# Evictions of the attention pass at a higher scheduler priority, with the copies of a key or query bank grouped ahead of its subtractions

## The chip, the cores and the metric

The kernel runs on one core of one Trainium2 chip. Its time is the device time in microseconds of one execution; 2264.72 us is the median of 3 runs (2261.97 to 2266.19). One execution was profiled by the hardware profiler; it took 2265.88 us, and its span, from the first recorded instruction to the last, is 2264.2 us.

## The reference

One layer of a hybrid encoder over 4096 tokens with 1024 channels. RMSNorm, one input projection, a group A of 4 heads (a matrix-memory recurrence in both directions), a group B of 8 query heads over 2 key/value heads (attention in a window of 128 tokens to either side), one output projection, a residual. Only group B is computed in the part of the kernel that the change touches:

```python
def windowed_gqa(q, k, v, sink, rel_bias):      # q [B,S,8,64], k, v [B,S,2,64]
    qb = q.reshape(bsz, nb, BLOCK, B_KV_HEADS, Q_PER_KV, B_HEAD_DIM)
    kw, vw = band(k), band(v)                   # the block before, this one, the next
    scores = jnp.einsum('bnqhgd,bnkhd->bnhgqk', qb, kw) * (B_HEAD_DIM ** -0.5)
...
    scores = jnp.where(mask[None, :, None, None], scores + bias, NEG_INF)
    m = jnp.maximum(jnp.max(scores, axis=-1), sink_l)
    p = jnp.exp(scores - m[..., None])
    denom = jnp.sum(p, axis=-1) + jnp.exp(sink_l - m)
    out = jnp.einsum('bnhgqk,bnkhd->bnqhgd', p, vw) / denom.transpose(0, 1, 4, 2, 3)[..., None]
```

## The kernel before

The kernel works in passes. Pass 1 (the first 700 us or so) normalizes and transposes x, projects queries, keys and values, and does the whole of the window attention; the passes behind it (the recurrence of group A, the output projection) are not touched by the change. At the end of pass 1 the weights of the next pass are loaded and split as well (`w2_load`), and the gates of group A are prepared (`gate1` to `gate3`).

Numbers are kept as a pair: a rounded high part and the rest as a low part, and products are three matmuls. So a TensorE result in a PSUM bank leaves it in two steps: ScalarE copies it (which rounds it, the high part), and VectorE subtracts that copy from the bank (the low part). This pair of steps is called an eviction here. Evictions of five kinds matter:

- xT (L358 copy, L359 subtraction): the transposed x, from the banks xtp.
- kk (L392, L393 copies, L394, L395 subtractions, each pair once for either key head): the keys, from kp. The program before writes copy, copy, subtraction, subtraction for head 0, then the same for head 1.
- vg (L415 copy, L416 addition): the values, from vp. From vg the value tile v is made (L419 on ScalarE, L420 on VectorE) and GpSimd adds the gate biases (L426).
- q (L449 copy, L450 subtraction, once for either half): the queries, from qp. Before: copy, subtraction, copy, subtraction.
- ab (L330 copy, L331 addition): the attention output, from op. After every second one a DMA stores ab to at_d, and there is one ab buffer.

The banks of xtp, kp, vp, qp and v2p come from one pool named pj of three PSUM banks, handed on from one tile to the next in the order in which they come free. A matmul that opens a new tile in a bank waits until the tile before in that bank has been evicted.

Attention itself, for each of 64 slots (a block of 128 queries by a key/value head): four pairs of score matmuls (sp, L276), VectorE adds the bias and takes the row maximum (L279, and L285 for the negated maximum), ScalarE takes four exponentials (L287) and one of the sink (L290), VectorE adds and inverts the row sums (L291, L292), GpSimd multiplies (L294), TensorE transposes the result (tp, L306), ScalarE and VectorE split it (pt, L308 and L309), and TensorE multiplies it with the values (op, L320).

What sets the order: the order of TensorE's instructions is that of the written program, in which `interleave` weaves the projections into the slots. The main loop runs 13 times (b = 0 to 12), each time four slots: first qproj of one block woven into two slots (the query half), then kproj and vproj of the next block and the transposes of a third woven into two slots (the key half). ScalarE, VectorE, GpSimd and the queue of SyncE, which issues most DMAs, get their order from the Tile scheduler: it takes, among the instructions that its own model says are ready, the one of highest priority, by default the earliest written. Each engine then works strictly through its list, and waits where an operand isn't there yet. If two engines touch one PSUM bank, the program lets one wait for the other.

`w2_load(j, c0)`, called three times near the end of pass 1, loads 8 tiles of weights through two staging buffers (tag xf) and splits each: most on ScalarE and VectorE (L470, L471), every fourth with GpSimd's help (L466 to L468). A staging buffer's next DMA goes out once its split has been done.

Of the kernel before, what the change touches and what calls it, by code (L numbers as in the profile page):

```python
# [12 lines left out]
AF = mybir.ActivationFunctionType  # L13
ALU = mybir.AluOpType
# [9 lines left out]
BIG = 1e30  # L24
BUCKET_STARTS = [0, 1, 2, 3, 4, 5, 6, 7, 8, 12, 16, 23, 32, 46, 64, 91]


def f32(ap):
    return ap.bitcast(F32)
# [133 lines left out]
def pass1(c):  # L163
    nc, tc, A = c.nc, c.tc, c.A
    NB = 16
    with ExitStack() as es:
# [144 lines left out]
        def att_o(sl, i):  # L311
            n, kv = sl // 2, sl % 2
# [5 lines left out]
            op, pt, vt = OP[sl], PT.pop((sl, i)), V[n - 1 + js[i]][:, kv, :]  # L318
# [7 lines left out]
            ab = AB[n]  # L326
            a = slice(0, 64) if kv == 0 else slice(64, 128)
            o = slice(64, 128) if kv == 0 else slice(0, 64)
            ov = op.rearrange("p (g q) -> p g q", g=4)
            nc.scalar.copy(ab[a], ov[o])  # L330
            nc.vector.tensor_add(ab[a], ov[a], ab[a])  # L331
# [14 lines left out]
        def transposes(b):  # L346
# [4 lines left out]
            def unit(kk):  # L351
# [6 lines left out]
                nc.scalar.copy(xt[:, :, 0, 2:], tp)  # L358
                nc.vector.tensor_tensor(out=xt[:, :, 1, 2:], in0=tp, in1=f32(xt[:, :, 0, 2:]), op=ALU.subtract)  # L359
# [13 lines left out]
        def kproj(b):  # L373
            R = {}

            def unit(k, j):
# [12 lines left out]
                for kv in range(2):  # L389
                    a = slice(kv * 64, kv * 64 + 64)  # L390
                    o = slice(64 - kv * 64, 128 - kv * 64)
                    nc.scalar.copy(kk[a, kv, 0, 256:512], kp[a, :])  # L392
                    nc.scalar.copy(kk[o, kv, 0, 256:512], kp[a, :])  # L393
                    nc.vector.tensor_sub(kk[a, kv, 1, 256:512], kp[a, :], f32(kk[a, kv, 0, 256:512]))  # L394
                    nc.vector.tensor_sub(kk[o, kv, 1, 256:512], kp[a, :], f32(kk[a, kv, 0, 256:512]))  # L395
# [3 lines left out]
        def vproj(b):  # L399
            R = {}  # L400

            def unit(i, k):
# [12 lines left out]
                nc.scalar.copy(vg, vp[:, 1, :])  # L415
                nc.vector.tensor_add(vg, vp[:, 0, :], vg)  # L416
# [14 lines left out]
        def qproj(b):  # L431
# [3 lines left out]
            def unit(m, k, j):  # L435
# [10 lines left out]
                for z in range(2):  # L446
                    a = slice(z * 64, z * 64 + 64)
                    o = slice(64 - z * 64, 128 - z * 64)
                    nc.scalar.activation(qt[a, z, :], qp[a, :], AF.Copy, scale=0.125)  # L449
                    nc.vector.scalar_tensor_tensor(qt[o, z, :], qp[a, :], 0.125, f32(qt[a, z, :]),  # L450
                                                   ALU.mult, ALU.subtract)
# [950 lines left out]
```

## Time and profile before

| | |
|---|---|
| median of 3 runs | 2264.72 us (2261.97 to 2266.19) |
| profiled execution, its own time | 2265.88 us |
| its span | 2264.2 us |
| TensorE (PE) busy in the span | 2210.4 us, 98% |
| VectorE (DVE) busy | 1492.3 us, 66% |
| ScalarE (ACT) busy | 1086.4 us, 48% |
| TensorE's share of the chain that ended last | 83% |
| granted TensorE clock, mean over the span | 0.995 |

The span is the time from the profiler's first event to its last; the execution's own time is 1.7 us more. Busy times are sums over all three passes, so the shares say little about one of them. In the rows below PE is TensorE's matmuls, PEld its weight loads, DVE VectorE, ACT ScalarE, POOL GpSimd, SP SyncE. A time in square brackets at the end of a row is how long the engine sat idle ahead of it, and what released it. "x4" at a row's end stands for four instructions of the same form that follow each other.

### The profile page before, as it was taken

To read this page: it belongs to the slowest core of one execution; us is meant where nothing else is said; L and a number is where in the kernel's file an instruction comes from. 1 tells how busy PE (TensorE), PEld (TensorE's weight loads), DVE (VectorE), ACT (ScalarE), POOL (GpSimd) and SP (SyncE) were. 2 spreads that over 40 slices of the span, in tenths; PEclk is the share of its full clock that TensorE was granted. 3 is DMA by queue.
4 is the path that set the end of the run, shared out by engine and by line. 5 is a ranking of instruction groups with operands and counts; after the bars stand their busy time and mean duration, and the time that the engine had idled before them with its cause. 6 is when DMAs were issued, how large, how long until landed. Compare 5 with 4: busy or idle time off the path is not lost.

```text
span 2264.2 us, 36115 instructions
## 1 busy us (share of the span) xinstructions
PE 2210.4 (98%) x12432; PEld 1914.0 (85%) x12432; DVE 1492.3 (66%) x3253; ACT 1086.4 (48%) x2710; POOL 617.2 (27%) x978
## 2 busy tenths in 40 slices
PE   7999999999989999999999999999999999999998
PEld 6999999999878888888887788888888888888887
DVE  5888888888877655655568554555554352766676
ACT  5777777777754333433345444434343331333332
POOL 2545454544532112211222111111111111122222
PEclk9999999999999999999999999999999999999999
DMA  8322222222225234432454986778676799466654
GB/s 235 122 98 99 99 99 99 98 99 80 74 86 159 88 109 152 157 109 88 155 191 132 311 244 226 212 232 254 222 223 200 268 365 311 148 168 167 167 169 129
DMA packets 257803, 376.08 MB, mean 166 GB/s; under 512 B 19507, under 2 KB 151219, under 8 KB 257620
## 3 DMA queue, kind: packets, MB, share of 16 engines
q1 hardware_dynamic: 238452, 307.90, 42.3%
q0 software_dynamic: 19024, 65.68, 9.5%
q8 instruction: 98, 1.61, 0.3%
q14 instruction: 85, 0.70, 0.1%
q10 hardware_dynamic: 144, 0.20, 0.0%
HBM read 253.18 MB, written 120.52 MB: 165 GB/s over the span
## 4 chain that ended last, share of the span: by engine, by line
PE 83%; DVE 7%; ACT 4%; DMA 3%; issue 2%; SPq 0%; POOL 0%; POOLq 0%; ACTq 0%; DVEq 0%
PE up L747 15%; PE o L1194 14%; PE op L1038 7%; PE zp L1038 7%; PE v2p L720 7%; PE qp L441 7%; PE zbp L153 3%; PE zbp L155 3%; PE zbp L154 3%; PE sp L276 3%; PE op L320 2%; PE tp L306 2%; PE num L991 2%; PE num L990 2%; ACT s L287 2%
## 5 line engine op out<-in xcount | busy, mean ns | idle before, releaser
L747 PE MATMUL up<-xb,w 128*128 128x512 f32 x1344 | 338.6, 396 | 0.0
L1194 PE MATMUL o<-wo,yo 128*128 128x512 f32 (+1 forms) x1356 | 312.1, 392 | 0.0
L1194 PEld LDWEIGHTS o<-wo,yo 128*128 128x128 f32 x1356 | 253.1, 188 | 59.1
L747 PEld LDWEIGHTS up<-xb,w 128*128 128x128 f32 x1344 | 243.9, 189 | 47.2
L294 POOL TENSOR_TENSOR s<-s,st 128x384 f32<-128x384 f32 (+1 forms) x256 | 203.9, 828 | 241.8 <-DVE st L292 191.1
L765 DVE SCALAR_TENSOR_TENSOR qk<-U,cw,qk 128x512 f32<-128x512 f32 x256 | 190.1, 755 | 93.0 <-ACT qk L763 89.2
L441 PE MATMUL qp<-xT,wqb 128*128 128x256 f32 x1536 | 248.3, 290 | 1.2 <-DVE xT L359 1.2
L441 PEld LDWEIGHTS qp<-xT,wqb 128*128 128x128 f32 x1536 | 221.8, 192 | 11.1 <-issue 1.7
L1038 PE MATMUL op<-w,xs 128*128 128x512 f32 x720 | 202.5, 408 | 1.1 <-DMA xs<-xT_d 1.1
L1038 PE MATMUL zp<-w,xs 128*128 128x512 f32 x720 | 187.9, 401 | 1.7 <-DVE z L1047 1.7
L287 ACT ACTIVATE s<-s,st 128x384 f32<-128x384 f32 (+1 forms) x256 | 152.9, 599 | 70.7 <-DVE st L285 70.7
L720 PE MATMUL v2p<-w,xb 128*128 128x512 f32 x672 | 157.2, 394 | 0.0
L1038 PEld LDWEIGHTS zp<-w,xs 128*128 128x128 f32 x720 | 130.7, 188 | 28.7 <-DVE z L1047 2.1
L720 PEld LDWEIGHTS v2p<-w,xb 128*128 128x128 f32 x672 | 126.1, 188 | 29.8 <-DMA xb<-xT_d 0.4
L1005 ACT ACTIVATE hs<-num,r 128x128 f32<-128x128 f32 x128 | 46.9, 367 | 209.6 <-DVE r L1002 171.5
L1038 PEld LDWEIGHTS op<-w,xs 128*128 128x128 f32 x720 | 126.5, 189 | 22.9 <-ACT hs L1005 1.6
L279 DVE CUSTOM_DVE_ANT_0 s<-sp,bias 128x384 f32<-128x384 f32 (+1 forms) x256 | 137.5, 541 | 12.5 <-PE sp L276 5.5
L276 PE MATMUL sp<-kk,q 128*128 128x384 f32 (+1 forms) x512 | 135.3, 345 | 2.1 <-DVE st L279 2.1
L309 DVE TENSOR_TENSOR pt<-tp,pt 128x512 fp32r<-128x512 f32 x188 | 128.2, 683 | 8.5 <-ACT pt L308 5.8
L320 PE MATMUL op<-pt,v 128*128 128x512 f32 x376 | 122.7, 408 | 6.2 <-DVE ab L331 5.8
L308 ACT CAST pt<-tp 128x512 fp32r<-128x512 f32 x188 | 109.1, 582 | 40.3 <-PE tp L306 37.3
L306 PE MATMUL tp<-ident,s 128*128 128x128 f32 x752 | 113.8, 273 | 2.5 <-DVE pt L309 2.0
(259 smaller groups left out, 4477.0 us busy)
## 6 DMA issues: line engine op xcount, KB each, us to landing
xT_d<-xT SPq DMA_DIRECT2D x128, 256.0 KB, 2.5
xc<-xT_d SPq DMA_DIRECT2D x64, 512.0 KB, 7.8
xs<-xT_d SPq DMA_DIRECT2D x120, 256.0 KB, 6.5
xb<-xT_d SPq DMA_DIRECT2D x48, 514.0 KB, 8.9
x<-x SPq DMA_DIRECT2D x32, 512.0 KB, 4.4
E<-m_d SPq DMA_DIRECT2D x64, 256.0 KB, 4.8
W<-w_d SPq DMA_DIRECT2D x64, 256.0 KB, 5.8
y<-y_d SPq DMA_DIRECT2D x32, 512.0 KB, 4.3
```

The source lines that it names most:

```text
L276: nc.tensor.matmul(sp[:, jl:jr], qt, kk[:, kv, z, col - 128 + jl:col - 128 + jr], start=(z == 0), stop=(z == 1))
L279: nc.vector.tensor_tensor_reduce(out=s[:, jl:jr], in0=sp[:, jl:jr], in1=bias[kv][:, g, jl:jr], op0=ALU.add, op1=ALU.max, scale=1.0, scalar ...
L287: nc.scalar.activation(ps[g][:, jl:jr], ps[g][:, jl:jr], AF.Exp, bias=ng[:, g:g + 1], accum_out=rs[:, g:g + 1])
L294: nc.gpsimd.tensor_tensor(out=ps[g][:, jl:jr], in0=ps[g][:, jl:jr], in1=rd[:, g:g + 1].broadcast_to([128, jr - jl]), op=ALU.mult)
L306: nc.tensor.transpose(tp[:, g * 128:(g + 1) * 128], ps[g][:, j * 128:(j + 1) * 128], c.ident)
L320: nc.tensor.matmul(op, vt, pt[:, z, :], start=(i == 0 and z == 0), stop=(i == len(js) - 1 and z == 1))
L441: nc.tensor.matmul(qp, wq[k // 2][:, k % 2, w, m * 128:m * 128 + 128], x[k], start=(k == 0 and j == 0), stop=(k == KT - 1 and j == 2))
L720: nc.tensor.matmul(vp, a, wv[k // 2][:, k % 2, m, :], start=(k == 0 and j == 0), stop=(k == KT - 1 and j == 2))
L747: nc.tensor.matmul(up[:, 0:hi - lo], w[k // 2][:, k % 2, a, cs], x, start=(k == 0 and j == 0), stop=(k == KT - 1 and j == 2))
L765: nc.vector.scalar_tensor_tensor(acc, U[:, t:t + 512], cw[:, cm, t:t + 1], acc, ALU.mult, ALU.add)
L1038: nc.tensor.matmul(P[nm], XS[n](a, k), w[:, m, :], start=(k == 0 and j == 0), stop=(k == KT - 1 and j == 2))
L1194: nc.tensor.matmul(p, a[:, z, k, :], w[k // 2][:, k % 2, m, lo:hi], start=k == 0 and z == 1, stop=k == 3 and z == 0 and m == 0)
```

## The change

The evictions ab, xT, kk, vg and q are written inside `tc.high_priority(offset=EV)` with EV = 400, which makes the scheduler rank them as if they had been written 400 places earlier. Further, the four ScalarE copies of a kk bank now come in front of its four VectorE subtractions, and the two copies of a q bank in front of its two subtractions. Instructions, shapes and the order on TensorE stay as they were.

```diff
+EV = 400
...
-            nc.scalar.copy(ab[a], ov[o])
-            nc.vector.tensor_add(ab[a], ov[a], ab[a])
+            with tc.high_priority(offset=EV):
+                nc.scalar.copy(ab[a], ov[o])
+                nc.vector.tensor_add(ab[a], ov[a], ab[a])
...
-                for kv in range(2):
-                    a = slice(kv * 64, kv * 64 + 64)
-                    o = slice(64 - kv * 64, 128 - kv * 64)
-                    nc.scalar.copy(kk[a, kv, 0, 256:512], kp[a, :])
-                    nc.scalar.copy(kk[o, kv, 0, 256:512], kp[a, :])
-                    nc.vector.tensor_sub(kk[a, kv, 1, 256:512], kp[a, :], f32(kk[a, kv, 0, 256:512]))
-                    nc.vector.tensor_sub(kk[o, kv, 1, 256:512], kp[a, :], f32(kk[a, kv, 0, 256:512]))
+                with tc.high_priority(offset=EV):
+                    for kv in range(2):
+                        a = slice(kv * 64, kv * 64 + 64)
+                        o = slice(64 - kv * 64, 128 - kv * 64)
+                        nc.scalar.copy(kk[a, kv, 0, 256:512], kp[a, :])
+                        nc.scalar.copy(kk[o, kv, 0, 256:512], kp[a, :])
+                    for kv in range(2):
+                        a = slice(kv * 64, kv * 64 + 64)
+                        o = slice(64 - kv * 64, 128 - kv * 64)
+                        nc.vector.tensor_sub(kk[a, kv, 1, 256:512], kp[a, :], f32(kk[a, kv, 0, 256:512]))
+                        nc.vector.tensor_sub(kk[o, kv, 1, 256:512], kp[a, :], f32(kk[a, kv, 0, 256:512]))
...
-                for z in range(2):
-                    a = slice(z * 64, z * 64 + 64)
-                    o = slice(64 - z * 64, 128 - z * 64)
-                    nc.scalar.activation(qt[a, z, :], qp[a, :], AF.Copy, scale=0.125)
-                    nc.vector.scalar_tensor_tensor(qt[o, z, :], qp[a, :], 0.125, f32(qt[a, z, :]),
-                                                   ALU.mult, ALU.subtract)
+                with tc.high_priority(offset=EV):
+                    for z in range(2):
+                        a = slice(z * 64, z * 64 + 64)
+                        o = slice(64 - z * 64, 128 - z * 64)
+                        nc.scalar.activation(qt[a, z, :], qp[a, :], AF.Copy, scale=0.125)
+                    for z in range(2):
+                        a = slice(z * 64, z * 64 + 64)
+                        o = slice(64 - z * 64, 128 - z * 64)
+                        nc.vector.scalar_tensor_tensor(qt[o, z, :], qp[a, :], 0.125, f32(qt[a, z, :]),
+                                                       ALU.mult, ALU.subtract)
```

The xT and vg evictions are only wrapped, as ab is. Lines of the changed kernel stand a little lower: L287 is L288, L290 is L291, L358 is L361, L392 and L393 are L396 and L397, L394 and L395 are L401 and L402, L449 is L458, L470 is L482.

The lists of the engines change with it. First ScalarE in the key half of one turn of the loop, before: kk_3734 is the key tile evicted here, kp_3627 its bank, s_0 to s_3 with st_3621 the four exponentials and the sums of one slot.

```order
L308 CAST pt_2_3729<-tp_2_3724 128x512
L392 CAST kk_3734<-kp_3627 64x256
L287 ACTIVATE s_0_3625,st_3621<-s_0_3625,st_3621 128x384
L287 ACTIVATE s_1_3640,st_3621<-s_1_3640,st_3621 128x384
L287 ACTIVATE s_2_3671,st_3621<-s_2_3671,st_3621 128x384
L287 ACTIVATE s_3_3697,st_3621<-s_3_3697,st_3621 128x384
L393 CAST kk_3734<-kp_3627 64x256
L290 ACTIVATE st_3621<-st_3621 128x4
L358 CAST xT_2_3772<-xtp_2_3767 128x2x256
L308 CAST pt_0_3782<-tp_0_3777 128x512
L415 COPY vg_3795<-vp_3750 128x144
L392 CAST kk_3734<-kp_3627 64x256
```

And the same place of ScalarE's list in the changed kernel:

```order
L309 CAST pt_2_3729<-tp_2_3724 128x512
L396 CAST kk_3734<-kp_3627 64x256
L397 CAST kk_3734<-kp_3627 64x256
L396 CAST kk_3734<-kp_3627 64x256
L397 CAST kk_3734<-kp_3627 64x256
L288 ACTIVATE s_0_3625,st_3621<-s_0_3625,st_3621 128x384
L288 ACTIVATE s_1_3640,st_3621<-s_1_3640,st_3621 128x384
L288 ACTIVATE s_2_3671,st_3621<-s_2_3671,st_3621 128x384
L288 ACTIVATE s_3_3697,st_3621<-s_3_3697,st_3621 128x384
L291 ACTIVATE st_3621<-st_3621 128x4
L361 CAST xT_2_3772<-xtp_2_3767 128x2x256
L309 CAST pt_0_3782<-tp_0_3777 128x512
```

The four copies of the key bank stood apart, one of them ahead of the slot's four exponentials and the others behind; now all four stand ahead of them.

VectorE at the same place, before:

```order
L309 TENSOR_TENSOR pt_2_3729<-tp_2_3724,pt_2_3729 128x512
L279 ISA s_5_3765,st_3744<-sp_5_3762,bias_326 128x384
L279 ISA st_3744 128x1
L394 TENSOR_TENSOR kk_3734<-kp_3627,kk_3734 64x256
L395 TENSOR_TENSOR kk_3734<-kp_3627,kk_3734 64x256
L291 TENSOR_TENSOR st_3621<-st_3621 128x4
L359 TENSOR_TENSOR xT_2_3772<-xtp_2_3767,xT_2_3772 128x2x256
L292 RECIPROCAL st_3621<-st_3621 128x4
L309 TENSOR_TENSOR pt_0_3782<-tp_0_3777,pt_0_3782 128x512
```

And in the changed kernel:

```order
L310 TENSOR_TENSOR pt_2_3729<-tp_2_3724,pt_2_3729 128x512
L401 TENSOR_TENSOR kk_3734<-kp_3627,kk_3734 64x256
L402 TENSOR_TENSOR kk_3734<-kp_3627,kk_3734 64x256
L401 TENSOR_TENSOR kk_3734<-kp_3627,kk_3734 64x256
L402 TENSOR_TENSOR kk_3734<-kp_3627,kk_3734 64x256
L280 ISA s_5_3765,st_3744<-sp_5_3762,bias_326 128x384
L280 ISA st_3744 128x1
L292 TENSOR_TENSOR st_3621<-st_3621 128x4
L293 RECIPROCAL st_3621<-st_3621 128x4
L362 TENSOR_TENSOR xT_2_3772<-xtp_2_3767,xT_2_3772 128x2x256
```

All four subtractions of the key bank now stand together, ahead of the score tile s_5 and of the transposed tile xT_2, which before came behind two of them. Which bank follows which changes too: the second value tile of a block (vp_3810 here) takes the bank of xtp_2 before, so that its first matmul waits for the xT_2 subtraction (L359); in the changed program it takes the bank of kp and waits for the last key subtraction (L402).

Last, ScalarE near the end of pass 1, where w_16 are weight tiles of `w2_load` whose data (w2s) come by DMA, and pt_2 belongs to the attention. Before:

```order
L470 ACTIVATE w_14_8845<-w2s_8851,nw 128x512
L330 COPY ab_8538<-op_8494 64x512
L308 CAST pt_2_8568<-tp_2_8563 128x512
L491 COPY v2t_8453<-v2p_8452 128x4x128
L470 ACTIVATE w_16_8855<-w2s_8856,nw 128x512
L555 ACTIVATE g_8581<-g_8581 128x256
```

And in the changed kernel:

```order
L309 CAST pt_1_8531<-tp_1_8526 128x512
L332 COPY ab_8538<-op_8494 64x512
L482 ACTIVATE w_16_8855<-w2s_8856,nw 128x512
L482 ACTIVATE w_16_8855<-w2s_8860,nw 128x512
L309 CAST pt_2_8568<-tp_2_8563 128x512
L503 COPY v2t_8453<-v2p_8452 128x4x128
```

Both splits of w_16 have moved ahead of the copy pt_2 (the second one stood behind four exponentials before). The same holds at two more places of this stretch: the second split of w_06 stands ahead of a pt_1 copy, and the first split of w_26 ahead of a v2t copy and the ab eviction that followed it.

## Rows read from the trace of the kernel before

**Rows 1.** The page: span, and busy time by engine.

```profile
span 2264.2 us, 36115 instructions
...
PE 2210.4 (98%) x12432; PEld 1914.0 (85%) x12432; DVE 1492.3 (66%) x3253; ACT 1086.4 (48%) x2710; POOL 617.2 (27%) x978
```

**Rows 2.** Busy time by stretch (stretch, length, engines, granted clock, DMA share, GB/s).

```profile
100.00:570.00 470.00, 461.55 (x3391) 439.00 (x3390) 413.24 (x1078) 352.05 (x946) 229.16 (x334) 1.00 0.28 94
570.00:700.00 130.00, 118.07 (x779) 105.67 (x778) 102.87 (x230) 79.63 (x187) 51.28 (x81) 0.97 0.25 78
```

**Rows 3.** Waits of all engines, 100 to 570 us (total us, times, longest).

```profile
DVE st L291 <- ACT st L290: 23.3, 25, 1.4
...
DVE kk L394 <- ACT kk L393: 8.1, 12, 0.7
PE vp L410 <- DVE xT L359: 7.5, 12, 0.6
...
PEld op L320 <- DVE ab L331: 3.1, 13, 0.7
```

**Rows 4.** TensorE in order of time, in one turn (start, us, what).

```profile
305.39 0.51 PE L276 MATMUL sp<-kk,q 128*128 128x384 f32 x2
305.74 0.52 PE L382 MATMUL kp<-xT,wkv 128*128 128x256 f32 x3
...
316.35 0.56 PE L276 MATMUL sp<-kk,q 128*128 128x384 f32 x2
317.55 0.40 PE L410 MATMUL vp<-wkv,xT 128*128 128x288 f32 x1 [0.64 <-DVE xT L359]
```

**Rows 5.** VectorE in order of time, same key half.

```profile
314.01 0.69 DVE L309 TENSOR_TENSOR pt<-tp,pt 128x512 fp32r<-128x512 f32 x1
...
315.85 0.42 DVE L394 TENSOR_TENSOR kk<-kp,kk 64x256 fp32r<-64x256 f32 x1 [0.68 <-ACT kk L393]
...
316.81 0.68 DVE L359 TENSOR_TENSOR xT<-xtp,xT 128x512 fp32r<-128x512 f32 x1
...
320.39 0.69 DVE L420 TENSOR_TENSOR v<-vg,v 128x128 fp32r<-128x128 f32 x1
...
322.68 0.67 DVE L359 TENSOR_TENSOR xT<-xtp,xT 128x512 fp32r<-128x512 f32 x1
```

**Rows 6.** ScalarE in order of time, same key half.

```profile
312.14 0.36 ACT L392 CAST kk<-kp 64x256 fp32r<-64x256 f32 x1
...
315.45 0.36 ACT L393 CAST kk<-kp 64x256 fp32r<-64x256 f32 x1
315.84 0.21 ACT L290 ACTIVATE st<-st 128x4 f32<-128x4 f32 x1
```

**Rows 7.** All v subtractions, 100 to 570 us (ns: least, median, most).

```profile
L420 DVE TENSOR_TENSOR v<-vg,v x25: 281/293/693, 99.8 to 552.8; 128x128 fp32r<-128x128 f32 x25
```

**Rows 8.** VectorE in the query half of the same turn.

```profile
307.63 0.16 DVE L291 TENSOR_TENSOR st<-st 128x4 f32<-128x4 f32 x1 [0.98 <-ACT st L290]
...
308.49 0.69 DVE L309 TENSOR_TENSOR pt<-tp,pt 128x512 fp32r<-128x512 f32 x1
```

**Rows 9.** TensorE's waits, 570 to 700 us.

```profile
PE op L320 <- DVE ab L331: 5.3, 6, 2.3
```

**Rows 10.** ScalarE near the end of pass 1.

```profile
600.15 0.73 ACT L470 ACTIVATE w<-w2s,nw 128x512 fp32r<-128x512 f32 x1 [0.20 <-DMA w2s<-w_in]
...
621.48 0.59 ACT L308 CAST pt<-tp 128x512 fp32r<-128x512 f32 x1
...
623.61 0.72 ACT L470 ACTIVATE w<-w2s,nw 128x512 fp32r<-128x512 f32 x1 [1.06 <-DMA w2s<-w_in]
...
651.18 0.58 ACT L330 COPY ab<-op 64x512 f32<-64x512 f32 x1
652.86 0.72 ACT L470 ACTIVATE w<-w2s,nw 128x512 fp32r<-128x512 f32 x1 [1.10 <-DMA w2s<-w_in]
...
657.41 0.58 ACT L330 COPY ab<-op 64x512 f32<-64x512 f32 x1 [2.56 <-DMA at_d<-ab]
```

**Rows 11.** VectorE at the pt_2 of rows 10.

```profile
624.19 0.67 DVE L309 TENSOR_TENSOR pt<-tp,pt 128x512 fp32r<-128x512 f32 x1
```

More of the change, by code (lines that the diff above doesn't have):

```diff
@@ L357, in unit @@
                 xt = xtile(c, [128, 2, 2, 258], F32R, f"xT{b}_{kk}")
-                nc.scalar.copy(xt[:, :, 0, 2:], tp)
-                nc.vector.tensor_tensor(out=xt[:, :, 1, 2:], in0=tp, in1=f32(xt[:, :, 0, 2:]), op=ALU.subtract)
+                with tc.high_priority(offset=EV):
+                    nc.scalar.copy(xt[:, :, 0, 2:], tp)
+                    nc.vector.tensor_tensor(out=xt[:, :, 1, 2:], in0=tp, in1=f32(xt[:, :, 0, 2:]), op=ALU.subtract)
                 if b == NB - 2:
@@ L414, in unit @@
                 vg = wk.tile([128, 144], F32, tag="vg", bufs=2, name=f"vg{n}")
-                nc.scalar.copy(vg, vp[:, 1, :])
-                nc.vector.tensor_add(vg, vp[:, 0, :], vg)
+                with tc.high_priority(offset=EV):
+                    nc.scalar.copy(vg, vp[:, 1, :])
+                    nc.vector.tensor_add(vg, vp[:, 0, :], vg)
                 vt = wk.tile([128, 2, 128], F32R, tag="v", bufs=7, name=f"v{n}")
@@ L445, in unit @@
                 qt = wk.tile([128, 2, 256], F32R, tag="q", bufs=6, name=f"q{b}_{m}")
-                for z in range(2):
-                    a = slice(z * 64, z * 64 + 64)
-                    o = slice(64 - z * 64, 128 - z * 64)
-                    nc.scalar.activation(qt[a, z, :], qp[a, :], AF.Copy, scale=0.125)
-                    nc.vector.scalar_tensor_tensor(qt[o, z, :], qp[a, :], 0.125, f32(qt[a, z, :]),
-                                                   ALU.mult, ALU.subtract)
+                with tc.high_priority(offset=EV):
+                    for z in range(2):
[7 more added lines that the diff above has]
+                                                       ALU.mult, ALU.subtract)
                 Q[b].append(qt)
```

## The prediction

> **What bounds the kernel now.** I began with the page. TensorE is busy for 98% of the span [rows 1], so no engine can be made to matter except where TensorE still waits; all its idle time together is 2264.2 - 2210.4 = 54 us. The table by stretch then says how much of it lies in pass 1, the only pass that the change touches: 470.0 - 461.55 = 8.5 us from 100 to 570 us, in the steady loop, and 130.0 - 118.07 = 11.9 us from 570 to 700, where the loads of the next pass's weights are mixed in [rows 2]. In the loop the granted clock is 1.00, the higher of its two levels (2.4 GHz), so nothing is to be had there from the clock. VectorE is the second engine: 413.24 of 470 us, 88%.
>
> The table of waits names what TensorE waits for in the loop: 7.5 us in 12 turns before the first matmul of a vp bank, on the xT subtraction, and 3.1 us in 13 times before the first op weight load of a slot, on ab [rows 3]. The first of them is the one that the change goes for. The view of TensorE in time gives its size in one turn: two score matmuls start at 316.35, and elsewhere the next matmul starts 305.74 - 305.39 = 0.35 behind such a pair, so vp would start at 316.70. It starts at 317.55 [rows 4]. The stall is 0.85 us a turn, 13 turns, 11 us.
>
> Why is xT late? VectorE has the answer in one row: after the pt subtraction of 314.01 and a score tile it stands idle for 0.68 us, until ScalarE's second key copy has come [rows 5]. That copy runs at 315.45 to 315.81, behind four exponentials, though ScalarE made the first one at 312.14 [rows 6]. So the chain in a turn is: exponentials, second key copy, two key subtractions, xT subtraction, vp.
>
> **The key half, changed.** ScalarE makes all four copies where it made one. They start at 312.14, and at 0.36 us each with 0.02 between them [rows 6] they are done by 313.65. The exponentials, and the sink's behind them, come about 0.73 later; it ended at 316.05 [rows 6] and now, no longer behind a key copy (0.36), ends near 316.4. VectorE starts its key subtractions behind the pt subtraction, at about 314.62, without a wait. Four of them at 0.42 with the step of 0.43 end near 316.35, before vp's natural start at 316.70. Since vp's bank is now that of kp, and not that of xtp_2, this is what vp waits for. The margin is 0.35 us, so the stall of 0.85 can go altogether.
>
> What is late next? VectorE takes the score tile (0.55) until 316.9 and needs the sink's exponential only then, when it has been there for 0.5. The sums, their inverse and xT_2 follow until 318.0, 0.5 later than now (316.81 + 0.68 = 317.49 [rows 5]). The transposes of xtp_3 wait for that one. They would start near 318.7, 0.85 sooner than in the trace, and have 0.7 to spare.
>
> TensorE can keep the gain only if VectorE, 88% busy, comes round sooner too. From the pt subtraction at 314.01 to the end of the turn's last xT subtraction (322.68 + 0.67) it does the same work as before, less the 0.68 of idleness. A second piece may go: the v subtraction takes 0.69 there [rows 5], while its 25 instances have a median of 0.293 [rows 7]. In the changed list it stands behind the copy of the old key tile. So VectorE gains between 0.68 and 0.68 + 0.39 = 1.07, and TensorE can use 0.85 of it. I take the middle of 0.68 and 0.85, 0.77: 13 x 0.77 = 10.0 us, with 8.8 and 11.1 as ends.
>
> The row of 0.69 against a median of 0.293 also has a rule beside it. The Trainium skill (SBUF — State Buffer, Who interferes with whom) says that VectorE with two SBUF inputs, or in a fast copy, shares a port pair with GpSimd as an exclusive lock, held for a whole instruction. By that rule the copy of the key tile, which now stands in the place of the v subtraction, would be held up in its stead, and the term would be its low end, 8.8 us, for a total 1.2 us higher than mine. No row of the trace of before has that copy in this place.
>
> **The query half, changed.** ScalarE's second q copy no longer waits for VectorE's first subtraction, but the last pair of q copies now stands between the exponentials of a slot, whose sink's exponential comes 2 x 0.37 = 0.73 later. VectorE already waits there 0.98 us [rows 8]. It can put both q subtractions (0.42 each) into that wait, which stood behind it before, around the pt subtraction of 308.49. The wait's end moves from 307.63 to 308.36, then the sums and the inverse until 308.76, then pt at about 308.8 to 308.9 in place of 308.49; but the q subtraction that followed it (0.45) is gone. The next score tile comes at 309.4 to 309.5 against 309.67. I set this at nothing; the cover is the 0.98 us of waiting, and without it the cost would be 0.73 a turn.
>
> **The other evictions.** Higher priority for xT, vg and ab moves single steps by one or two places. The v tiles move back behind ab, but are first used by later slots, tens of microseconds on. Passes 2 and 3 keep their order. I put these and the first 100 us at nothing; another turn's wait or two there would be 1 us.
>
> **The end of pass 1.** Here the change puts instructions that wait for a DMA ahead of evictions, on an engine that works in order. Three places:
> - The second w_06 split waits for its data until 600.15 [rows 10]. Now a pt copy (0.59, about 0.5 from start to start) stands between it and ab: ab 0.5 later. TensorE already waits for ab there; the longest of the 5.3 us in 6 waits is 2.3 [rows 9].
> - Both w_16 splits stand ahead of pt_2. The first is held by its data until 623.61 [rows 10], the second ends about 624.9, and pt_2 is copied 3.4 us later than at 621.48. VectorE reached pt_2 only at 624.19 [rows 11]; it will now be 624.9 + 0.5 = 625.4, 1.2 later, on the engine that TensorE waits for next.
> - The first w_26 split is held until 652.86, and ab, copied at 651.18, now comes behind it and behind a v2t copy, at 654.1: 2.9 later. Its load goes out some 0.6 earlier, as the splits ahead of it have moved before a pt copy. That leaves 2.3. The last ab waits 2.56 for the store of this one [rows 10], and moves with it.
> Sum: 0.5 + 1.2 + 2.3 = 4.0 us. At best all this is hidden (0). At worst each is paid in full, with another split (0.6) ahead of a pt copy: 0.5 + 3.4 + 2.9 + 0.6 = 7.4. I take 4.0, since TensorE waits for the evictions at each of these places in the trace.
>
> **Sum.** 2265.9 (the profiled execution) - 10.0 + 4.0 = 2259.9. That execution lies 1.2 us over the median, so against the median it is 2258.7 us. The ends of the terms give 2265.9 - 11.1 + 0 - 1.2 = 2253.6 and 2265.9 - 8.8 + 7.4 - 1.2 = 2263.3. About 0.2% (4.5 us) is what a measurement of this kernel can tell from no change: 2260.2 to 2269.2 counts as the same.
>
> **Rivals.**
> - More than the vp stall goes. If VectorE gains the full 1.07, the wait on ab goes too (3.1 / 13 = 0.24 a turn). With the end of pass 1 hidden: 13 x 1.09 = 14.2 less, 2250.5 at the median. For it: the v subtraction's 0.69. Against it: the ab wait lies before the part that is shortened. 0.12.
> - Given back. VectorE's lead is used up by its waits for the sink's exponential, 23.3 us in 25 times in the loop [rows 3]. With half of the 0.77 lost so, 13 x 0.38 = 5.0 less and 4.0 more: 2263.7 at the median, the same. For it: ScalarE now has copies ahead of or between the exponentials in both halves of a turn. Against it: both have cover above. 0.25.
> - Slower, by the same wait in full. VectorE works in order, so whatever delays the sink's exponential holds up its xT and pt subtractions too. If neither cover holds, each half of a turn loses 0.73: 13 x (1.46 - 0.77) + 4.0 = 13 more, 2276.5 at the median. It decides from new waits of more than 0.77 + 0.5 / 13 = 0.81 us a turn on. Against it: the 0.98 us of idle time that VectorE can fill. 0.11.
> - That the change does nothing at all is excluded by the lists: the copies and subtractions do stand in other places.
>
> **Chances and range.** My forecast has 0.52, of which its own range, 2253.6 to 2263.3, crosses into the same at 2260.2; about a fifth (0.10) falls there. The rival above (0.12) adds to faster, the given-back case to the same. In sum faster 0.54, same 0.35, slower 0.11. The range that holds 8 in 10 reaches from 2250 (the first rival) to 2267 (the given-back case with the whole 7.4 at the end of pass 1, 2263.7 + 3.4); the slow rival lies outside.
>
> **What the profile will show.** Right, if the wait of vp on xT is gone from the table of waits, if VectorE's wait of 0.68 before the key subtractions is gone, and if TensorE's idle time between 100 and 570 us, of 8.5 us, loses most of the 7.5 that the wait of vp makes up (the drain of TensorE ahead of each stall counts as busy, so the time gained is more than that). In the end part I expect new ScalarE waits on w2s ahead of pt_2 and ab, and a longer op wait on ab than 5.3 us in all. I am wrong if the wait of VectorE for the sink's exponential grows by more than it loses at the key copies, or if vp now waits as long for the key subtractions as it did for xT.

## The result

The changed kernel takes 2250.16 us in the median of 5 runs (2248.69 to 2253.45), the kernel before 2263.46 us in 5 runs beside it (2261.97 to 2266.19). The ratio is 0.9941, with a 95% interval of 0.9927 to 0.9954: 13.3 us faster. The forecast was 6.0 us (2264.7 to 2258.7). The time lies 0.2 us inside the lower end of the stated range (2250), and below the 2253.6 that the forecast's own terms reach.

The page of the changed kernel, as [rows 1]: 14.4 us less span, of which TensorE's busy time gives 9.8 and its idle time 4.6. VectorE is busy for 27.5 us less, with the same number of instructions.

```profile
span 2249.8 us, 36150 instructions
...
PE 2200.6 (98%) x12432; PEld 1912.0 (85%) x12432; DVE 1464.8 (65%) x3253; ACT 1094.3 (49%) x2710; POOL 628.8 (28%) x978
```

TensorE's list is the same in both kernels, so each of its matmuls can be sought in both traces, and the difference of the two starts says how far the changed kernel is ahead there. At 100 us of the trace of before it is 1.0 us ahead, at 560 us (the end of the loop) 15.5, at 664 us (the end of pass 1) 15.7, at 740 us 14.5, at 2200 us 14.4. So the loop wins 14.5 us, the end of pass 1 gives 0.2, and 1.2 us are lost at the start of the next pass, where TensorE runs dry twice (0.38 and 0.45 us) behind a load of xb.

The stretch of eleven turns of the loop between the same two matmuls, first of the kernel before, in the columns of [rows 2]:

```profile
127.03:542.03 415.00, 407.17 (x2994) 387.12 (x2993) 365.84 (x950) 311.54 (x837) 202.88 (x297) 1.00 0.29 99
```

And of the changed kernel:

```profile
125.48:527.28 401.80, 400.58 (x2994) 386.51 (x2993) 342.82 (x951) 318.28 (x837) 212.77 (x297) 1.00 0.30 102
```

The turns are 13.2 us shorter, 1.20 us each. TensorE's idle time is almost gone: 7.8 us before, 1.2 now. The rest of the 13.2 us had been counted as busy, as a part of each stall is: in [rows 4] the step to vp is 0.85 us longer than elsewhere, and 0.64 of that are marked as idle. And VectorE does the same 950 instructions in 23 us less.

The waits of the same eleven turns in the kernel before, with which those of the experiments below can be compared:

```profile
PEld vp L410 <- DVE xT L359: 10.4, 11, 1.0
DVE kk L394 <- ACT kk L393: 7.4, 11, 0.7
PE vp L410 <- DVE xT L359: 6.9, 11, 0.6
PEld op L320 <- DVE ab L331: 3.0, 12, 0.7
PE op L320 <- DVE ab L331: 0.6, 1, 0.6
```

The table of waits from 100 to 570 us, as [rows 3], of the changed kernel. The rows of vp waiting for xT and of VectorE waiting for a key copy aren't there any more. VectorE's wait for the sink's exponential, the row on which two of the rivals hung, has fallen from 23.3 to 17.2 us. New is VectorE waiting for TensorE: it has time now. The waits on ab have become fewer, 3 in place of 13, but one of them is longer than any before.

```profile
DVE st L292 <- ACT st L291: 17.2, 13, 2.8
...
DVE s L280 <- PE sp L277: 11.9, 18, 1.0
...
PEld op L321 <- DVE ab L333: 1.8, 3, 1.4
PE op L321 <- DVE ab L333: 1.2, 1, 1.2
```

The key half of the same turn in time, as [rows 4 to 6]. ScalarE of the changed kernel makes its four copies and then the exponentials:

```profile
304.69 0.36 ACT L396 CAST kk<-kp 64x256 fp32r<-64x256 f32 x1
...
305.82 0.37 ACT L397 CAST kk<-kp 64x256 fp32r<-64x256 f32 x1
306.09 0.61 ACT L288 ACTIVATE s<-s,st 128x384 f32<-128x384 f32 x1
...
308.50 0.20 ACT L291 ACTIVATE st<-st 128x4 f32<-128x4 f32 x1
```

VectorE comes to the key bank from its pt subtraction without a wait, and to the sums without one either:

```profile
305.87 0.69 DVE L310 TENSOR_TENSOR pt<-tp,pt 128x512 fp32r<-128x512 f32 x1
306.47 0.40 DVE L401 TENSOR_TENSOR kk<-kp,kk 64x256 fp32r<-64x256 f32 x1
...
307.76 0.43 DVE L402 TENSOR_TENSOR kk<-kp,kk 64x256 fp32r<-64x256 f32 x1
...
308.73 0.16 DVE L292 TENSOR_TENSOR st<-st 128x4 f32<-128x4 f32 x1
...
309.34 0.69 DVE L362 TENSOR_TENSOR xT<-xtp,xT 128x512 fp32r<-128x512 f32 x1 [0.24 <-ACT xT L361]
```

And TensorE goes from the score matmuls to vp in 0.39 us, against 1.20 in [rows 4]. The last key subtraction is over at 308.19, 0.9 us ahead of that vp; xT_2, for which vp waited before, ends at 310.03 and would be late.

```profile
308.68 0.56 PE L277 MATMUL sp<-kk,q 128*128 128x384 f32 x2
309.07 0.29 PE L417 MATMUL vp<-wkv,xT 128*128 128x288 f32 x1
```

VectorE's 23 us show in one line of code above all, the negated maximum of a slot (128 x 4 elements). The groups by line over the eleven turns (busy us, mean ns, idle before), first of the kernel before, then of the changed one:

```profile
L285 DVE SCALAR_TENSOR_TENSOR st<-st,nsink 128x4 f32<-128x4 f32 x44 | 24.6, 560 | 1.1
```

```profile
L286 DVE SCALAR_TENSOR_TENSOR st<-st,nsink 128x4 f32<-128x4 f32 x44 | 7.0, 159 | 1.1
```

One of the four of a turn took 1.79 us before, at 332.47 of that trace; GpSimd's normalizing multiplication of a block of x had begun at 332.35 and takes 1.89 us:

```profile
332.35 1.89 POOL L207 TENSOR_TENSOR x<-x,rstd 128x1024 f32<-128x1024 f32 x1
332.47 1.79 DVE L285 SCALAR_TENSOR_TENSOR st<-st,nsink 128x4 f32<-128x4 f32 x1
```

In the changed kernel that instruction runs at 323.96 for 0.16 us, and the multiplication begins at 323.98. VectorE isn't free of it, though: the next small instruction of the slot, the sum for the sink's exponential (L290), is caught in both kernels, here for 1.14 us, and its line takes 19 us of the eleven turns before and after.

```profile
323.96 0.16 DVE L286 SCALAR_TENSOR_TENSOR st<-st,nsink 128x4 f32<-128x4 f32 x1
323.98 1.91 POOL L208 TENSOR_TENSOR x<-x,rstd 128x1024 f32<-128x1024 f32 x1
324.76 1.14 DVE L290 TENSOR_TENSOR st<-sink,st 128x4 f32<-128x4 f32 x1
```

At the end of pass 1 two waits of TensorE have grown, that of op on ab and that of the gates of group A (gp), and the one of tp on a pt subtraction is gone. First the two rows of the kernel before that [rows 9] leaves out, from 545 to 700 us, then the changed kernel from 560 to 700:

```profile
PE gp L583 <- DVE G L565: 2.2, 1, 2.2
PE tp L306 <- DVE pt L309: 2.0, 3, 1.3
```

```profile
PE op L321 <- DVE ab L333: 6.7, 5, 2.5
PE gp L595 <- DVE G L577: 4.4, 1, 4.4
```

### The profile page after: what moved, and what is told of

Read it like the earlier page. It is cut to its first block, busy times and chain, and to the rows that moved or that the text cites. A ratio compares the mean times of both kernels' runs of the same rounds, so it can differ in the third digit from the quotient of the medians.

```text
span 2249.8 us, 36150 instructions
## 1 busy us (share of the span) xinstructions
PE 2200.6 (98%) x12432; PEld 1912.0 (85%) x12432; DVE 1464.8 (65%) x3253; ACT 1094.3 (49%) x2710; POOL 628.8 (28%) x978
## 4 chain that ended last, share of the span: by engine, by line
PE 89%; DMA 4%; DVE 3%; ACT 2%; issue 1%; SPq 0%; POOL 0%; POOLq 0%; DVEq 0%; ACTq 0%
PE up L759 15%; PE o L1206 14%; PE zp L1050 7%; PE op L1050 7%; PE qp L449 7%; PE v2p L732 7%; PE op L321 4%; PE sp L277 4%; PE tp L307 3%; PE zbp L154 3%; PE zbp L156 3%; PE zbp L155 3%; PE num L1003 2%; PE num L1002 2%; PE kp L385 2%; PE vp L417 2%
## 5 line engine op out<-in xcount | busy, mean ns | idle before, releaser
L449 PE MATMUL qp<-xT,wqb 128*128 128x256 f32 x1536 | 246.6, 289 | 0.2 <-DVE xT L362 0.2
L449 PEld LDWEIGHTS qp<-xT,wqb 128*128 128x128 f32 x1536 | 220.1, 191 | 9.5 <-issue 1.1
L288 ACT ACTIVATE s<-s,st 128x384 f32<-128x384 f32 (+1 forms) x256 | 153.1, 600 | 28.6 <-DVE st L286 27.9
```

The costliest lines, as they stand in the source:

```text
L288: nc.scalar.activation(ps[g][:, jl:jr], ps[g][:, jl:jr], AF.Exp, bias=ng[:, g:g + 1], accum_out=rs[:, g:g + 1])
L449: nc.tensor.matmul(qp, wq[k // 2][:, k % 2, w, m * 128:m * 128 + 128], x[k], start=(k == 0 and j == 0), stop=(k == KT - 1 and j == 2))
```

## The experiments

Theory 1 is that of the prediction: what is won is the stall of vp, through the key bank, and the end of pass 1 costs something. Theory 2 came from the trace after: VectorE's loop as a whole was late, and it lost its time beside GpSimd. All ratios are against runs of the kernel before on the same chip; those medians lie between 2263.46 and 2268.30 us. In the table below each column says how far the same matmul of TensorE is ahead of the trace of before, at that time of the trace of before, in one profiled execution each; the last column is the change of the median. From 740 to 2200 us, in passes that the change does not touch, these single executions still differ from that of before by anything from 0.3 us won to 4.5 lost; so what is won or lost in a part of the program is read from the columns before, and the total from the medians.

| kernel | 100 us | 560 us | 664 us | 2200 us | median, us |
|---|---|---|---|---|---|
| whole change | 1.0 | 15.5 | 15.7 | 14.4 | -13.3 |
| whole change, again | 0.3 | 14.4 | 13.5 | 11.2 | -14.1 |
| key part alone | 4.1 | 16.2 | 21.1 | 18.7 | -17.7 |
| all but the key part | -0.6 | 6.9 | 7.3 | 4.0 | -2.8 |
| before, GpSimd cut in four | 0.1 | 5.7 | 6.0 | 3.7 | -4.1 |
| key grouped, no priority | 2.1 | -24.8 | -19.8 | -20.1 | +18.2 |
| priority, no grouping | -1.7 | 3.0 | 3.7 | 0.6 | -6.1 |
| key part, GpSimd cut in four | 3.3 | 15.5 | 23.3 | 17.4 | -18.0 |
| key part, query priority | 3.9 | 15.7 | 21.8 | 20.1 | -20.5 |
| the same, again | 3.4 | 15.1 | 21.8 | 21.8 | -22.5 |
| the same, query grouped in the loop | 3.7 | 19.4 | 26.7 | 24.9 | -23.5 |

**The key part alone.** Only kk is grouped and raised:

```diff
+                with tc.high_priority(offset=EV):
                     for kv in range(2):
...
                         nc.scalar.copy(kk[a, kv, 0, 256:512], kp[a, :])
                         nc.scalar.copy(kk[o, kv, 0, 256:512], kp[a, :])
+                    for kv in range(2):
...
                         nc.vector.tensor_sub(kk[a, kv, 1, 256:512], kp[a, :], f32(kk[a, kv, 0, 256:512]))
                         nc.vector.tensor_sub(kk[o, kv, 1, 256:512], kp[a, :], f32(kk[a, kv, 0, 256:512]))
```

> Only the key bank is changed: its four copies, then its four subtractions, at the higher priority; ab, xT, vg and q as before. Theory 1 (the prediction): the 0.85 us stall of vp is what is won, by this part alone, so the time falls by 9 to 11 us and the end of pass 1 keeps its order; TensorE's waits on ab (0.26 a turn) and in the score matmuls (0.20 a turn) stay. Theory 2: VectorE's loop as a whole is late, largely because small VectorE instructions sit beside GpSimd's normalization (L285 took up to 1.79 us before, at most 0.49 after), and the key part only brings it out of that place: then all of TensorE's waits in the loop go, 13 to 15 us, and L285 is short here too. If that place is left because of the query part, L285 stays long here and the gain is 9 us or less.

Measured: 2248.61 us, ratio 0.9920 (0.9906 to 0.9933), 17.7 us less. That is more than the whole change wins, and more than any of the three amounts that the two theories had named. The loop wins 12.1 us. The line of the negated maximum is nearly as long as before, and still TensorE's wait of vp on xT is gone from the loop's table. The waits on ab stay, fewer and longer. The group by line and the waits over the same eleven turns:

```profile
L286 DVE SCALAR_TENSOR_TENSOR st<-st,nsink 128x4 f32<-128x4 f32 x44 | 22.5, 510 | 1.1
```

```profile
PEld op L321 <- DVE ab L332: 2.8, 6, 1.0
PE op L321 <- DVE ab L332: 1.5, 3, 0.8
```

So the key part alone carries the loop, and leaving the place next to GpSimd isn't needed for it: Theory 2 falls as the cause, and Theory 1 sized the loop too small. The start (4.1 us) and the end of pass 1 (4.9 us) win too, which neither theory had.

**All but the key part.** The whole change, with the kk block as in the kernel before (no wrapping, copy, copy, subtraction, subtraction).

> The whole change except the key bank, which is evicted as before. Theory 1: vp waits for xT_2 as before, nothing is won in the loop, and the end of pass 1 costs 0 to 4 us: the same time as before to 4 us more. Theory 2, with the query part as what moves VectorE away from GpSimd's normalization: L285 is short, VectorE is 1.6 us a turn earlier, and 5 to 12 us are won without any change of the key bank.

Measured: 2263.54 us, ratio 0.9984 (0.9976 to 0.9993), 2.8 us less: between the two theories, outside the range of either. The negated maximum is short here, and vp still waits for xT in every turn, only less long than before (4.1 us against 6.9). The group by line and the waits over the eleven turns:

```profile
L286 DVE SCALAR_TENSOR_TENSOR st<-st,nsink 128x4 f32<-128x4 f32 x44 | 6.9, 158 | 1.1
```

```profile
PEld vp L413 <- DVE xT L362: 7.6, 11, 0.7
DVE kk L397 <- ACT kk L396: 6.9, 11, 0.6
PE vp L413 <- DVE xT L362: 4.1, 11, 0.4
```

Without the key part the loop wins 7.5 us this way in the profiled execution. The first 100 us lose 0.6, and 3.3 more are gone between 664 and 2200 us, 2.3 of them in the passes that the change does not touch.

**The kernel before, with GpSimd's multiplication cut in four.**

```diff
-                nc.gpsimd.tensor_tensor(out=xs[i], in0=xs[i], in1=rstd[:, i:i + 1].broadcast_to([128, D]), op=ALU.mult)
+                for h in range(4):
+                    xp = xs[i][:, h * 256:h * 256 + 256]
+                    nc.gpsimd.tensor_tensor(out=xp, in0=xp, in1=rstd[:, i:i + 1].broadcast_to([128, 256]), op=ALU.mult)
```

> The kernel before, with each of GpSimd's two normalizing multiplications of a block cut into four over 256 columns; all other lists as before. Theory 1: VectorE's long small instructions lie in the query half, where it has time, so the time stays (within 2 us). Theory 2: the long ones shrink from 1.79 and 1.21 us to about a quarter of a whole multiplication (0.5 us), VectorE comes round 1 to 2 us a turn sooner, the vp stall shrinks to 0.2 or less, and 8 to 13 us are won with no change of the evictions.

Measured: 2262.24 us, ratio 0.9982 (0.9973 to 0.9991). The longest negated maximum falls from 1.79 to 0.51 us, and the group to less than half of the 24.6 us:

```profile
L287 DVE SCALAR_TENSOR_TENSOR st<-st,nsink 128x4 f32<-128x4 f32 x44 | 10.8, 245 | 1.1
```

So VectorE's long instructions were waits for the end of a GpSimd instruction, and cutting that into pieces gives most of it back. It is worth 5.5 us in the loop and 4.1 in the median: more than the 2 us of Theory 1, about half of what Theory 2 expected. VectorE still waits for the second key copy in every turn (6.8 us in the eleven), and vp for xT (4.3 us).

**The key bank grouped, with no priority.** The diff of the key part without the `with` line.

> Only the writing order of the key bank is changed (four copies, then four subtractions), with no higher priority: three of the four copies still come behind the four exponentials, and all four subtractions still ahead of xT_2. Theory 1: VectorE still waits for a copy (0.68 and two more copies, 0.7, since the last subtractions now need the fourth copy), vp waits for the last key subtraction instead of xT_2, which ends about as late: within 3 us of before. Theory 2: the same for the wait, and a gain only if L285 comes out short.

Measured: 2284.51 us, ratio 1.0079 (1.0066 to 1.0091), 18.2 us slower; both theories had put it within a few us of before. In the waits over the eleven turns vp now waits for the last key subtraction, and VectorE waits twice as long for the copies:

```profile
PEld vp L413 <- issue: 22.7, 11, 2.1
...
PE vp L413 <- DVE kk L398: 19.6, 11, 1.8
DVE kk L397 <- ACT kk L393: 15.8, 11, 1.4
```

The grouping moves vp to the bank of kp, and all four subtractions ahead of xT_2, as in the changed kernel. But three of the four copies stay behind the exponentials, and so what vp now waits for is late: the step to vp takes about 2 us longer than without a wait, against 0.85 before. The same grouping costs 18.2 us without priority and brings 17.7 with it.

Not all of that is waiting. The granted clock of the eleven turns is 0.97, against 1.00 in all other runs: in eight short stretches of the loop it falls to the lower of its two levels, 1.2 GHz (stretch, length, engines, granted clock as in [rows 2], one of the eight):

```profile
168.22:171.62 3.40, 3.40 (x15) 3.10 (x14) 2.07 (x7) 2.04 (x4) 3.09 (x4) 0.50 0.22 77
```

By the matched matmuls each of the eight costs 1.4 to 1.6 us, 12.0 in all. The longer step to vp costs 13.5 us in the eleven turns. Together that is nearly the whole of the 26.9 us that the loop loses; the start and the end of pass 1 give some of it back.

**Priority without grouping.** All five evictions raised, but kk and q in the old writing order.

> All evictions at the higher priority, but a key or query bank in its old writing order (copy, copy, subtraction, subtraction; copy, subtraction, copy, subtraction). In its lists two key copies stand ahead of the exponentials, two behind; VectorE takes the first two key subtractions early, then the sums, xT_2, and only then the last two; vp still takes the bank of xtp_2 and waits for xT_2. Theory 1 (the wait of 0.68 goes, whatever the bank): xT_2 ends about 0.4 us sooner, vp's stall falls from 0.85 to 0.45 a turn, 4 to 7 us are won. Theory 2 (the gain is that vp hangs on the key bank, which is done before xT_2): the vp wait on xT_2 stays in the table with 12 turns, at half its size, and far less is won than the 17.7 us of the key part alone. Rival: the last two subtractions come so late that xtp_3, which takes the bank of kp, waits for them, and nothing is won.

Measured: 2260.47 us, ratio 0.9975 (0.9966 to 0.9985), 6.1 us less, within what Theory 1 said. It does not decide between the two: vp still waits for xT_2 in every turn, as Theory 2 said, 4.1 us in all at the weight loads against 10.4 before, and far less is won than by the key part alone.

```profile
PEld op L321 <- DVE ab L333: 4.3, 10, 0.9
PEld vp L414 <- DVE xT L362: 4.1, 11, 0.4
```

The waits on ab have grown, from 3.0 us to 4.3. Its first 100 us are 1.7 us slower, and it loses 3 us behind pass 1; its single profile lies above its median.

**The key part with the query bank raised but not grouped.** The key part, and the q block inside `high_priority` with copy, subtraction, copy, subtraction. Beside it stands a fact of the lists: the key part with the grouped query part has the lists of the whole change on ScalarE and VectorE, instruction for instruction. The priority of ab, xT and vg changes nothing beside these two. (For the loop the traces show it too: the run below with the query bank grouped in the loop has these three unraised, and there ScalarE and VectorE go through the same order as in the whole change.)

> The key part (four copies, four subtractions, higher priority) with the query bank at higher priority but in its old writing order. The lists of the key part with the query part as the change has it are those of the whole change, instruction for instruction, so the query part alone accounts for what the whole change wins less than the key part (17.7 against 13.3 us). If the grouping of the query bank is what costs, this kernel has the key part's time, 16 to 19 us under before; if the priority of the query bank is what costs, it has the whole change's, 12 to 15 us under.

Measured: 2246.04 us, ratio 0.9911 (0.9898 to 0.9925), 20.5 us less, and 2245.76 us, 0.9904 (0.9888 to 0.9921), when run again beside the last one below. Both are above the 16 to 19 us expected, and well away from the 12 to 15. So the grouping of the query bank is what costs. The table shows where: about 3 us in the first 100, and 6 to 8 at the end of pass 1, while it wins 2 to 4 in the loop.

At the end of pass 1 TensorE waits for gp. VectorE of the changed kernel there has two weight splits ahead of the gate result G:

```profile
626.08 2.03 DVE L483 SCALAR_TENSOR_TENSOR w<-w2s,nw,w 128x512 fp32r<-128x512 f32 x2
628.04 0.82 DVE L577 SCALAR_TENSOR_TENSOR G<-g 128x256 f32<-128x256 f32 x1
```

With the query bank raised but not grouped they stand behind it, and gp waits 1.47 us and not 4.37:

```profile
623.98 0.41 DVE L571 SCALAR_TENSOR_TENSOR G<-g 128x256 f32<-128x256 f32 x1
624.32 1.40 DVE L477 SCALAR_TENSOR_TENSOR w<-w2s,nw,w 128x512 fp32r<-128x512 f32 x2
```

That is 2.9 us of the 6 to 8. The waits of op on ab are 3.3 us fewer as well (3.4 against 6.7), those of tp on a pt subtraction 1.9 more. And the granted clock from the end of the loop to the end of pass 1 is 0.97 in the changed kernel, in both its runs, and 1.00 here.

**The key part with GpSimd cut in four.** Both edits above together.

> The key part alone, with GpSimd's normalizing multiplications cut into four as in the run before. If VectorE's long small instructions (L285 with 22 us in 11 turns) still hold TensorE up in the key part's loop, up to the 0.31 us a turn that is left of the waits on ab goes, 2 to 4 us more than the key part alone. If VectorE now has slack, nothing changes: within 2 us of the key part alone.

Measured: 2248.58 us, ratio 0.9923 (0.9911 to 0.9936), the same as the key part alone (2248.61). With the key part VectorE has slack, and its time next to GpSimd is hidden.

**The whole change again**, on the same chip as the last three.

> The changed kernel as it is, on the same chip and against the same runs of before as the other three: 12 to 15 us under before, and 2 to 6 us over the key part alone.

Measured: 2252.50 us, ratio 0.9936 (0.9922 to 0.9949), 14.1 us less. The key part with the query bank raised but not grouped was 6.5 us faster than this beside it.

**The query bank grouped in the loop only.** The key part, with ab, xT and vg as before, and in the q block, with cp a copy and sb a subtraction:

```diff
+                with tc.high_priority(offset=EV):
+                    for f, z in ((cp, 0), (cp, 1), (sb, 0), (sb, 1)) if 2 <= b <= 13 else ((cp, 0), (sb, 0), (cp, 1), (sb, 1)):
+                        f(z)
```

> The key part, with the query bank at higher priority, and grouped (both copies ahead of both subtractions) only for blocks 2 to 13; blocks 0, 1, 14 and 15 in the old writing order. Its lists are those of the whole change in the loop and those of the run with query priority alone at the start and the end. Theory 1 (what the grouping costs, it costs outside the loop: about 3 us before 100 us and 5 to 7 at the end of pass 1, where VectorE splits two weight tiles ahead of the gate result that TensorE waits for): the loop's 14 us are kept and the rest comes back, 19 to 24 us under before, that is 6 to 9 under the whole change and at or under the key part alone. Theory 2 (where TensorE stands when the loop ends decides what the end costs): with the loop of the whole change the end costs what it costs there, 13 to 16 us under before.

And of its partner in the same run:

> The key part with the query bank at higher priority in its old writing order, once more beside the run above: 19 to 22 us under before. If the grouping in the loop gives back VectorE's time next to GpSimd's normalization (17 us in 11 turns there), the run above is up to 2 us faster than this one; if TensorE already sets the pace of the loop, they are within 1 us.

Measured: 2244.83 us, ratio 0.9892 (0.9877 to 0.9906), 23.5 us less, the fastest of all kernels here. It keeps the loop of the whole change (15.7 us won between 100 and 560 us) and the start and end of its partner, as Theory 1 of that run said; where TensorE stands at the end of the loop doesn't decide. The profiled execution is the fastest of its runs. Against the partner's 2245.76 us it is not clearly faster by the runs: the intervals overlap. The waits of TensorE from 560 to 700 us, to compare with those of the changed kernel:

```profile
PE op L321 <- DVE ab L332: 3.5, 3, 1.5
...
PE gp L588 <- DVE G L570: 1.5, 1, 1.5
```

## Why the prediction was right, and where its sizes were off

**What landed, and how.** The mechanism came true: the four copies early, vp on the key bank, the stall gone. The sizes didn't. The loop won 4.5 us more than its term, and the end of pass 1 cost 4.2 less. Both errors go the same way, so the time left the forecast's own ends and reached the range only by what the first rival had added to it. That it lies inside, by 0.2 us, is in part luck.

**The key half: right in its mechanism, too small.** All its steps show in the rows: the copies at the front, VectorE without its wait, vp on the key bank, the sink's exponential covered, xT_2 later but not missed. The key part alone is enough for it. The term was 10.0 us, and the loop won 14.5. Where it was won can be read from the matched matmuls: the time from the start of one to the start of the next, summed by kind of step over the eleven turns, in us won against the kernel before.

| step of TensorE | whole change | key part alone | all but the key part | before, GpSimd cut in four | priority, no grouping |
|---|---|---|---|---|---|
| from the score matmuls to vp, and between the two matmuls of a vp pair | 9.8 | 9.8 | 2.8 | 2.6 | 6.3 |
| from vp to op, which waits for ab | 2.7 | 2.2 | 2.7 | 2.7 | 2.2 |
| between score matmuls, and from qp to them | 1.6 | 1.6 | 1.6 | 1.6 | -0.1 |
| from qp to op, and between the op | -0.9 | -1.8 | 0.2 | -1.7 | -4.1 |
| all | 13.2 | 11.8 | 7.2 | 5.2 | 4.3 |

The stall of vp was sized well: 9.8 / 11 = 0.89 us a turn, against the 0.85 measured and the 0.77 taken. The limit was wrong: TensorE was allowed the stall of vp alone, as the only one that the key bank touches. But VectorE and TensorE form one loop. Whichever way VectorE gains time, by the key part, by the query part or by shorter GpSimd instructions, the small wait of op behind vp goes, 0.20 to 0.25 us a turn, and in all but the last column some time at the score matmuls as well. Against that stand a few new waits of op behind qp. That the wait on ab goes is what the first rival said (0.24 a turn), at 14.2 us for the loop. It got 0.12 because the ab wait lies ahead of the shortened part; in a loop, ahead is also behind.

**VectorE's gain: missed in kind.** The prediction gave VectorE 0.68 to 1.07 us a turn. In the changed kernel it has 23.0 / 11 = 2.1 us of busy time less, on top of the 0.68 of idleness. The v subtraction gives the 0.37 that was the prediction's upper end. Most is the negated maximum, 17.6 / 11 = 1.6 us a turn, for which the prediction had no row. But the runs say that it wasn't needed: the key part alone has the long instructions, and with them shortened its loop is no faster (12.1 and 12.2 us won).

**The rule beside the v subtraction.** By the Trainium skill (SBUF — State Buffer, Who interferes with whom) the copy of the old key tile could have been held up in place of the v subtraction. It wasn't: its 12 instances take 677 to 682 ns, as before, and no v subtraction takes more than 294 ns, against 693 in [rows 7]; the term's low end did not come. The collision is there all the same, and GpSimd is the one that is held up. Before, no GpSimd instruction ran beside that copy. In the changed kernel one of the four small additions of the gate biases runs beside each, and takes about 1.1 us, where none took more than 0.27 before. All of these additions from 100 to 560 us, before and changed (ns: least, median, most):

```profile
L426 POOL TENSOR_TENSOR G<-vg,gb x96: 196/203/266, 132.5 to 551.9; 128x4 f32<-128x4 f32 x96
```

```profile
L434 POOL TENSOR_TENSOR G<-vg,gb x96: 195/203/1162, 130.2 to 535.9; 128x4 f32<-128x4 f32 x96
```

What the rule says of a lock held for a whole instruction agrees with that and with the negated maximum: 1.79 us beside a multiplication of 1.89, at most 0.51 when that is cut in four.

**The query half: set at nothing, but it wins in the loop and costs outside.** In the loop it wins 2 to 4 us, by the runs with and without its grouping, at the waits of op on ab; how it shortens these was not followed. It is not by the negated maximum, as the key part with GpSimd cut in four shows. At the start it costs about 3. A part of that shows between 40 and 60 us, where TensorE waits once for a score tile: 2.9 us in the changed kernel and 2.0 when it was run again, 1.4 and 1.2 with the query bank raised, 0.2 with the key part alone (2.1 before). In the two runs of the changed kernel the granted clock then falls to its lower level for a short stretch (at 48.5 and 50.9 us), and with the key part alone or with the query bank raised it stays at 1.00 there. If that costs what it cost in the run with no priority, 1.4 to 1.6 us, the two together come near the 3; this is an estimate, not a run.

**The end of pass 1: its signs came, the sum did not.** The term was 4.0 us more; measured, 0.2 less, and 0.9 more when run again. As expected, ScalarE waits longer for w2s (4.6 us against 3.4) and op longer for ab (6.7 us against 5.3). But where pt_2 was to cost 1.2 us, the waits of tp on a pt subtraction, 2.0 us before, are gone. And the gate result behind two splits on VectorE, 2.2 us more than before, is a cost that the prediction did not have. Splits ahead of evictions need not cost: in the lists of the key part alone they have also moved ahead of pt copies, and its end wins 4.9 us. The key part's gain and the query part's loss there nearly cancel, so that the small sum is chance.

**The rivals.** "Given back" failed at its row: the waits for the sink's exponential became fewer. The slower rival's mechanism, a late ScalarE in front of the in-order VectorE, isn't in the changed kernel, but a near relative is in the grouping without priority, at 18.2 us. (Its price was added up wrongly: 13 us over the median of 2264.7 are 2277.7, not 2276.5.)

**Left open.** The 1.2 us behind pass 1 are not in every run (none in the key part alone, 0.9 when the change was run again), and were not pursued. Nor were the few new waits of op on ab in the loop, of up to 1.4 us, and why the key part alone wins at the start, where its waits between 40 and 60 us are 2.6 us shorter than before.

## What to carry to other kernels

When two engines empty one bank in several steps, look for the copy that stands behind unrelated work in the first engine's list, and check which later tile takes that bank: the same regrouping cost 18 us where the copies stayed behind the exponentials, a good part of it by the clock, and won 18 where they came ahead. In a loop of two nearly full engines count the other small waits of the first one as winnable by slack in the second too, not only the wait that ends at the edited place. And try the parts of a change apart: the key bank carried this one, three raised evictions changed nothing, and the grouping of the query bank took about a third of the gain away (14.1 us against 20.5 side by side), all of it outside the loop.

## What the runs showed of the hardware

A VectorE instruction on 128 x 4 elements took 0.16 us alone and up to 1.79 us when it began 0.12 us behind a GpSimd multiplication of 1.89 us; when it began 0.02 us ahead of one, it took 0.16. With GpSimd's work cut into four, the longest was 0.51 us, and the kernel before became 4.1 us faster by that alone. The other way round, a GpSimd addition on 128 x 4 elements, 0.20 us in the median, took about 1.1 us beside a VectorE copy of 0.68.

In the run in which vp waited for the key bank, TensorE stood still for about 2 us in each turn, and its granted clock fell from 2.4 to 1.2 GHz in eight short stretches of the loop. These cost 12.0 us of the 26.9 that the loop lost. With the stall of 0.85 us a turn, in the kernel before, the clock stayed at 1.00 through the loop.
